# w_down in block products with sums by VectorE, gated factors stored as hi and lo, two weight sums of gate and up by adding transfers

## The chip, the cores and the metric

One core of a Trainium2 chip runs the whole kernel as one program. The metric is device microseconds (us) of that core. An execution under the profiler gives the span from the first to the last instruction, and its own time beside it.

## What is computed

An encoder block for 512 tokens of width 2048 in float32: a normalisation, eight projections, four mLSTM heads and eight differential attention heads, an output projection, and then the gated channel mixer that this case is about. Its width D_FF is 5632.

```python
x = x + jnp.concatenate([hm, ha], axis=-1) @ w_out[l]
h2 = rmsnorm(x, norm2_g[l])
x = x + (jax.nn.silu(h2 @ w_gate[l]) * (h2 @ w_up[l])) @ w_down[l]
return rmsnorm(x, final_g)
```

## The kernel before, in words

**Three matmuls for one.** Every float32 factor is split into a rounded half `hi` and a rest `lo` (`split`, L96): ScalarE (ACT) casts it (L98), VectorE (DVE) subtracts (L99). `three` (L157) then multiplies hi by hi, hi by lo and lo by hi on TensorE (PE). Weights arrive by transfers of SyncE's queue (SP) as tiles of 128 x 1024 in the ring `raw` (7 buffers) and are split into the rings `whi` and `wlo` (3 buffers each), two factors ahead of the product that uses them (`factor`, L921).

**Gate and up.** For each of 22 blocks of 256 features, `group` (L961) runs once for w_gate and once for w_up: 44 groups. A group is a 2 x 2 block product in Winograd's form: seven products P1, P6, P7, P5, P2, P4, P3 of 24 matmuls (128 x 256 out, L931 to L933), with sums around them. `left_factors` (L851) makes the seven weight factors of a group: it loads the four blocks (L856), forms four sums with VectorE (L871, L872, L873, L881) and yields each factor split. `after` (L974) adds the products up with VectorE (L972). `up` (L1032) multiplies with the silu of the gate. For the first 16 blocks it forms four more sums (L1043 to L1046) and writes seven variants of the gated factor to the HBM tensor `actv` by transfers of GpSimd's queue (POOL; L1048, L1049). The last 6 blocks go to `actd` (L1035).

**Down.** w_down's first 4096 rows are worked in 8 units u = (ci, dg), four parts of rows by two halves of columns, in a loop at L1069. A unit is seven products of 24 matmuls (128 x 512 out, L1067, recorded at L158 to L160); each product takes two weight factors, h = 0 and 1, of 12 matmuls each. `load` (L885) fetches the two plain blocks and makes three block sums by a transfer and a second, adding one of GpSimd's queue (L889, L891); two more sums are VectorE's (L913, L915). The left factors are the variants: `variant` (L946) loads one as float32 into a ring `ra` of 2 buffers (L956) and splits it, in the odd units (dg = 1) one product's worth for the next ci beside each product. Products are added over ci into the tiles `M` (L1088 by ScalarE for ci = 0, then L1090 by VectorE).

**The end.** `combine` (L1097) forms the output from the `M` tiles and adds the residual by adding transfers (L1106). The last 1536 rows of w_down are plain products: four blocks by `proj_tok` (L162, called at L1198) and two in the last loop (L1212), which also normalises and stores.

A scheduler sets the order of each engine's instructions; each engine and each queue then works in that order.

Of the kernel before, what the change touches and what calls it, by code (L numbers as in the profile page):

```python
# [30 lines left out]
def build(nc, tc, ctx, a, out):  # L31
# [11 lines left out]
    pacc = pool("acc", 4, space=bass.MemoryType.PSUM)  # L43
    paux = pool("aux", 4, space=bass.MemoryType.PSUM)
# [23 lines left out]
    def tacc():  # L68
        return pacc.tile([128, 512], F32, tag="acc", name=nm("acc"))

    def taux():
        return paux.tile([128, 512], F32, tag="aux", name=nm("aux"))
# [763 lines left out]
    actd = dram.tile([NFB, 2, 128, 512], F32, name="actd")  # L836
    actv = dram.tile([4 * NSP, 7, 128, 256], F32, name="actv")
# [7 lines left out]
    DOWN = ["P1", "P3", "P6", "P5", "P7", "P4", "P2"]  # L845
# [5 lines left out]
    def left_factors():  # L851
        def loads(w, g):
            r = []
            for q in range(4):
                t = tW("raw", bufs=7)
                nc.sync.dma_start(t, a[w][g, q])  # L856
                r.append(t)
            return r
# [8 lines left out]
        for i in range(len(todo)):  # L867
            w11, w12, w21, w22 = nxt
            yield parts(w11)
            s1 = tW("raw", bufs=7)  # L870
            V.tensor_tensor(s1, w21, w22, ALU.add)  # L871
            V.tensor_tensor(w21, w11, w21, ALU.subtract)  # L872
            V.tensor_tensor(w11, s1, w11, ALU.subtract)  # L873
            yield parts(w11)
            yield parts(w21)
# [5 lines left out]
            V.tensor_tensor(w12, w12, w11, ALU.subtract)  # L881
# [3 lines left out]
        def load(u, h, i, ring):  # L885
            j, n, j2, n2 = ((0, 0, 0, 0), (1, 1, 1, 1), (0, 0, 0, 1), (1, 1, 0, 1), (1, 0, 1, 0))[i]
            ci, dg = divmod(u, 2)
            t = ring()
            nc.sync.dma_start(t, a["w_ds"][ci, dg, j, n, h])  # L889
# [4 lines left out]
        order = [(u, i, h) for u in range(2 * NSP) for i in range(5) for h in range(2)]  # L894
# [3 lines left out]
        def upto(k):  # L898
            while pos[0] < min(k, len(order)):
                u, i, h = order[pos[0]]  # L900
                got[u, i, h] = load(u, h, i, tR if h and (u, i) != (0, 0) else lambda: tW("raw", bufs=7))
                pos[0] += 1

        upto(2)
        for u in range(2 * NSP):
            k = 10 * u
            for pi, name in enumerate(DOWN):
                if u or pi:
                    upto(k + (14 if pi == 0 else 16 if pi < 6 else 20))
                for h in range(2):  # L910
                    B11, B22, T1, T3, B21 = (got.get((u, i, h)) for i in range(5))
                    if name == "P6":
                        V.tensor_tensor(B22, B22, T1, ALU.add)  # L913
                    if name == "P4":
                        V.tensor_tensor(B22, B22, B21, ALU.add)  # L915
                    yield parts({"P1": B11, "P3": B22, "P6": B22, "P5": T1, "P7": T3, "P4": B22, "P2": B21}[name])
# [28 lines left out]

    def variant(ci, name, into):  # L946
# [3 lines left out]
        for h in range(2):  # L950
            if more:
                r = more[2].tile([128, 512], F32, tag="ra", name=nm("ra"), bufs=2)
            else:
                r = tW("raw", bufs=7)[:, 0:512]
            g0 = 4 * ci + 2 * h
            nc.sync.dma_start(r.rearrange("p (g c) -> p g c", g=2), actv[g0:g0 + 2, v].rearrange("g p c -> p g c"))  # L956
            hi, lo = tA(), tA()
            split(hi, lo, r)
            into[name].append((hi, lo))

    def group(scale, done, first=False, last=False):  # L961
# [11 lines left out]

        def after(name):  # L974
            if name == "P1":
                SC.copy(ps[:, L], banks[name])
            if name == "P6":
                add(u[:, L], name, ps[:, L])
            if name == "P7":
                add(u[:, R], name, u[:, L])  # L980
            if name == "P5":
                add(C2[:, R], name, u[:, R])
                add(ps[:, R], name, u[:, L])
            if name == "P2":
                add(C1[:, L], name, ps[:, L])
            if name == "P4":
                add(C2[:, L], name, u[:, R])
# [36 lines left out]
    for g in range(NFB):  # L1024
# [7 lines left out]
        def up(i, t):  # L1032
            V.tensor_tensor(t, t, sl[i], ALU.mult)
            if g >= 4 * NSP:
                G.dma_start(actd[g, i], t)  # L1035
# [16 lines left out]
        group(None, up, last=g == NFB - 1)  # L1052


    late[0].close()
    mst, (pM,) = stage(("mm", 1),)
    more.extend(stage(("rr", 1), ("ra", 1)))
    more[1:] = more[1]
    M = [{}, {}]

    def product_down(banks, w, name, h):
        for m in range(2):
            rs = slice(m * 512, m * 512 + 512)
            hi, lo = got_v[name][h]
            for tt in range(2):
                ts = slice(m * 256 + tt * 128, m * 256 + tt * 128 + 128)
                three(banks[tt], hi[:, ts], lo[:, ts], w[0][:, rs], w[1][:, rs], h == 0 and m == 0, h == 1 and m == 1)  # L1067

    for u in range(2 * NSP):  # L1069
        ci, dg = divmod(u, 2)  # L1070
        got_v = cur_v
        if dg == 1:
            cur_v = {}
        for pi, name in enumerate(DOWN):
            if u == 0 and pi < 3:
                variant(0, DOWN[4 + pi], cur_v)
            if dg == 1 and ci + 1 < NSP:
                variant(ci + 1, name, cur_v)
            banks = [tacc(), taux()]
            for h in range(2):  # L1080
                product_down(banks, factor(), name, h)
# [245 lines left out]
```

## Time and profile before

| | us |
|---|---|
| median of 3 runs (2181.03 to 2182.97) | 2181.36 |
| the profiled execution, its own time | 2190.05 |
| span of the profiled execution | 2188.3 |
| PE busy | 2142.0 |
| DVE busy | 1569.6 |
| ACT busy | 992.7 |
| POOL busy | 133.8 |

The profiled execution's own time is 1.75 us longer than its span. The profile counts a matmul as busy until its modelled end, so PE's busy time includes matmuls that run at a lower granted clock. Registers, semaphores and the waiting of the queues are not busy time. By the products' lines, gate and up run from about 800 us to 1693 us, the units of w_down to about 2043 us, and the rest to the end.

### The profile page before, as it was taken

What the parts mean: (1) busy time and instruction counts of PE and PEld (TensorE: products, weight loads), DVE (VectorE), ACT (ScalarE), POOL (GpSimd) and SP (SyncE); (2) the same over time, 40 slices, a digit from 0 to 9 for tenths busy, and PEclk for the clock granted to TensorE, in tenths of its full rate; (3) what the DMA queues carried; (4) which work ended last, traced back from release to release, by engine and by line L of the source; (5) the groups of instructions that cost most, each with busy time, mean ns of one, the idle gap of its engine ahead of it and who ended that gap; (6) DMA issues with size and microseconds to landing.
All of it is one profiled execution on the core that took longest, in us unless ns stands there. A gap on an engine that the chain in (4) does not pass through costs nothing.

```text
span 2188.3 us, 33437 instructions
## 1 busy us (share of the span) xinstructions
PE 2142.0 (98%) x13305; PEld 1938.2 (89%) x13305; DVE 1569.6 (72%) x2362; ACT 992.7 (45%) x1515; POOL 133.8 (6%) x189
## 2 busy tenths in 40 slices
PE   9999999999999999999999999999999799999998
PEld 7888889988888889999999999999999577778786
DVE  6267776366544468888888888888889467779745
ACT  6256675355434354344344443343444454444423
POOL 0011110000000000000000000000000000001100
PEclk9999999999999999999999999999999999999999
DMA  6232112332234424343443434433335986876732
GB/s 257 96 96 78 62 53 72 116 97 87 82 112 146 140 92 131 124 145 119 129 135 119 137 121 133 131 123 117 121 121 168 284 228 184 242 210 156 203 106 77
DMA packets 100749, 292.56 MB, mean 134 GB/s; under 512 B 10976, under 2 KB 27376, under 8 KB 100592
## 3 DMA queue, kind: packets, MB, share of 16 engines
q1 hardware_dynamic: 86832, 247.42, 34.5%
q0 software_dynamic: 13760, 43.00, 8.4%
q8 instruction: 104, 1.70, 0.3%
q14 instruction: 53, 0.43, 0.1%
HBM read 264.16 MB, written 26.22 MB: 133 GB/s over the span
## 4 chain that ended last, share of the span: by engine, by line
PE 85%; DMA 6%; DVE 6%; ACT 2%; issue 1%; ACTq 0%; POOL 0%; DVEq 0%; SPq 0%; POOLq 0%
PE acc L159 9%; PE acc L158 9%; PE acc L160 9%; PE acc L933 8%; PE acc L932 8%; PE acc L931 8%; PE aux L933 6%; PE aux L932 6%; PE aux L931 6%; DMA ra<-actv 4%; PE acc L189 4%; PE acc L190 4%; PE acc L191 4%; DVE wlo L99 2%; PE aux L160 1%
## 5 line engine op out<-in xcount | busy, mean ns | idle before, releaser
L98 ACT CAST whi<-raw 128x1024 fp32r<-128x1024 f32 (+2 forms) x573 | 593.6, 1037 | 807.4 <-PE acc L932 238.8
L99 DVE TENSOR_TENSOR wlo<-raw,whi 128x1024 fp32r<-128x1024 f32 (+2 forms) x573 | 690.5, 1206 | 305.8 <-ACT whi L98 295.0
L158 PE MATMUL acc<-whi,A 128*128 128x512 f32 (+1 forms) x1056 | 404.0, 384 | 21.4 <-ACT whi L98 18.2
L159 PE MATMUL acc<-wlo,A 128*128 128x512 f32 (+1 forms) x1056 | 403.7, 382 | 9.5 <-DVE wlo L99 9.5
L160 PE MATMUL acc<-whi,A 128*128 128x512 f32 (+1 forms) x1056 | 400.7, 379 | 0.0
L158 PEld LDWEIGHTS acc<-whi,A 128*128 128x128 f32 x1056 | 200.0, 190 | 59.4 <-ACT whi L98 22.5
L159 PEld LDWEIGHTS acc<-wlo,A 128*128 128x128 f32 x1056 | 200.3, 190 | 48.0 <-DVE wlo L99 15.0
L160 PEld LDWEIGHTS acc<-whi,A 128*128 128x128 f32 x1056 | 200.4, 190 | 34.0
L932 PE MATMUL acc<-A,whi 128*128 128x256 f32 x704 | 199.3, 283 | 0.5 <-DVE A L99 0.5
L931 PE MATMUL acc<-A,whi 128*128 128x256 f32 x704 | 199.4, 283 | 0.0
L931 PE MATMUL acc<-h,whi 128*128 128x256 f32 x704 | 199.4, 283 | 0.0
L933 PE MATMUL acc<-h,wlo 128*128 128x256 f32 x704 | 199.2, 283 | 0.0
L932 PE MATMUL acc<-h,whi 128*128 128x256 f32 x704 | 199.2, 283 | 0.0
L933 PE MATMUL acc<-A,wlo 128*128 128x256 f32 x704 | 199.2, 283 | 0.0
L933 PE MATMUL aux<-h,wlo 128*128 128x256 f32 x528 | 149.7, 284 | 0.8 <-DVE wlo L99 0.8
L931 PE MATMUL aux<-h,whi 128*128 128x256 f32 x528 | 149.6, 283 | 0.6 <-ACT whi L98 0.6
L189 PE MATMUL acc<-A,whi 128*128 128x512 f32 x384 | 150.1, 391 | 0.0
L190 PE MATMUL acc<-A,whi 128*128 128x512 f32 x384 | 149.8, 390 | 0.0
L191 PE MATMUL acc<-A,wlo 128*128 128x512 f32 x384 | 149.8, 390 | 0.0
L933 PE MATMUL aux<-A,wlo 128*128 128x256 f32 x528 | 149.4, 283 | 0.0
L931 PE MATMUL aux<-A,whi 128*128 128x256 f32 x528 | 149.4, 283 | 0.0
L932 PE MATMUL aux<-A,whi 128*128 128x256 f32 x528 | 149.4, 283 | 0.0
(280 smaller groups left out, 4123.9 us busy)
## 6 DMA issues: line engine op xcount, KB each, us to landing
raw<-in_w_g_dram SPq DMA_DIRECT2D x88, 512.0 KB, 3.5
raw<-in_w_u_dram SPq DMA_DIRECT2D x88, 512.0 KB, 3.6
raw<-in_w_ds_dram SPq DMA_DIRECT2D x80, 512.0 KB, 5.1
raw<-in_w_aqk_dram SPq DMA_DIRECT2D x32, 512.0 KB, 3.4
raw<-in_w_o_dram SPq DMA_DIRECT2D x32, 512.0 KB, 3.5
raw<-in_w_ds_dram POOLq DMA_DIRECT2D x32, 512.0 KB, 8.2
raw<-in_w_b_dram SPq DMA_DIRECT2D x31, 512.0 KB, 4.0
actv<-x POOLq DMA_DIRECT2D x48, 256.0 KB, 3.4
```

The costliest lines, as they stand in the source:

```text
L98: SC.copy(hi, src)
L99: V.tensor_tensor(lo, src, hi.bitcast(F32), ALU.subtract)
L158: PE.matmul(acc, lh, rh, start=first, stop=False)
L159: PE.matmul(acc, lh, rl, start=False, stop=False)
L160: PE.matmul(acc, ll, rh, start=False, stop=last)
L189: PE.matmul(banks[f], wh[:, cs], xh[k], start=first, stop=False)
L190: PE.matmul(banks[f], wh[:, cs], xl[k], start=False, stop=False)
L191: PE.matmul(banks[f], wl[:, cs], xh[k], start=False, stop=last)
L931: PE.matmul(bank, w[0][:, cs], hi, start=m == 0, stop=False)
L932: PE.matmul(bank, w[0][:, cs], lo, start=False, stop=False)
L933: PE.matmul(bank, w[1][:, cs], hi, start=False, stop=m == 7)
```

## The change

1. Gate and up: two of a group's four weight sums are no longer VectorE's. `s1` and `s3` are made by a transfer of SP's queue and an adding one of POOL's into the same tile; the signs of the sums are turned so that only additions are needed. A group now loads five tiles and adds into two of them. VectorE keeps two sums (L879, L887 of the changed file). In the built program a group's s3 takes, of the seven `raw` buffers, the one that the previous group's s3 left; its load can start when that one has been split.
2. The gated factors: each variant, and each of the last 6 blocks, is split into hi and lo when it is made (`halves`, `keep`, L1045 to L1078), and both halves are stored in HBM. The pieces of work wait in a list `later` and run after P1, P6, P7 and P2 of the following group.
3. Down: `variant` loads hi and lo straight into the tiles that the products read, 28 tiles for each ci out of a ring of 38. A table NEXT sets beside which product. No adding transfer is left here: each unit loads four blocks of two tiles and VectorE makes four sums (L916). The order of the products is P1, P5, P3, P7, P2, P6, P4.
4. P1 is added over ci in PSUM (`p1`) and never copied out; the other products use two pairs of banks (`pair`), each copied or added in one instruction of 1024 columns (L1148, L1150).
5. The end: the four blocks for `proj_tok` are loaded during the last units, already split; `combine` becomes a generator in four steps for each half; the splits of the last weights are spread over more steps.

```diff
@@ acc and aux were fixed pools of 4 PSUM banks each @@
+    psum = list(banks_of(("acc", 4), ("aux", 4)))
...
@@ def left_factors(): @@
-            for q in range(4):
+            for q, q2 in ((0, None), (2, 3), (0, 2), (1, None), (3, None)):
                 t = tW("raw", bufs=7)
                 nc.sync.dma_start(t, a[w][g, q])
+                if q2 is not None:
+                    G.dma_start(t, a[w][g, q2], accum_op=ALU.add)
                 r.append(t)
...
-            w11, w12, w21, w22 = nxt
+            w11, s1, s3, w12, w22 = nxt
             yield parts(w11)
-            s1 = tW("raw", bufs=7)
-            V.tensor_tensor(s1, w21, w22, ALU.add)
-            V.tensor_tensor(w21, w11, w21, ALU.subtract)
-            V.tensor_tensor(w11, s1, w11, ALU.subtract)
+            V.tensor_tensor(w11, w11, s1, ALU.add)
             yield parts(w11)
-            yield parts(w21)
+            yield parts(s3)
             yield parts(s1)
             if i + 1 < len(todo):
                 nxt = loads(*todo[i + 1])
             yield parts(w12)
             yield parts(w22)
-            V.tensor_tensor(w12, w12, w11, ALU.subtract)
+            V.tensor_tensor(w12, w12, w11, ALU.add)
             yield parts(w12)
...
-            j, n, j2, n2 = ((0, 0, 0, 0), (1, 1, 1, 1), (0, 0, 0, 1), (1, 1, 0, 1), (1, 0, 1, 0))[i]
...
-            if (j, n) != (j2, n2):
-                G.dma_start(t, a["w_ds"][ci, dg, j2, n2, h], accum_op=ALU.add)
+            j, n = ((0, 0), (0, 1), (1, 1), (1, 0))[i]
+            t = tR() if (h if u else i > 1) else tW("raw", bufs=7)
+            nc.sync.dma_start(t, a["w_ds"][u // 2, u % 2, j, n, h])
             return t
...
+        upto(4)
         for u in range(2 * NSP):
...
-                    upto(k + (14 if pi == 0 else 16 if pi < 6 else 20))
+                    upto(8 * u + (8, 8, 8, 10, 10, 12, 14)[pi])
...
+                    t, o = {"P1": (B11, None), "P5": (B11, B12), "P3": (B22, None), "P7": (B12, B22),
+                            "P2": (B21, None), "P6": (B11, B22), "P4": (B21, B11)}[name]
+                    if o is not None:
+                        V.tensor_tensor(t, t, o, ALU.add)
+                    yield parts(t)
...
@@ def variant(ci, name, into): @@
-            nc.sync.dma_start(r.rearrange("p (g c) -> p g c", g=2), actv[g0:g0 + 2, v].rearrange("g p c -> p g c"))
-            hi, lo = tA(), tA()
-            split(hi, lo, r)
-            into[name].append((hi, lo))
+            into[name].append((tAA(), tAA()))
+            for p in range(2):
+                nc.sync.dma_start(into[name][h][p].bitcast(F32), actv[p, v, 2 * ci + h])
...
@@ def after(name): @@
+            if later and name in ("P1", "P6", "P7", "P2"):
+                later.pop(0)()
...
@@ def up(i, t): @@
+            def halves(t):
+                hi, lo = tX(F32R)[:, :t.shape[1]], t.bitcast(F32R)
+                split(hi, lo, t)
+                return hi, lo
...
-            for k, t in ((0, C1), (2, C2), (4, Sa)):
-                G.dma_start(actv[g, k:k + 2].rearrange("v p c -> p v c"), t.rearrange("p (v c) -> p v c", v=2))
-            G.dma_start(actv[g, 6], Sb[:, L])
+            def keep(k, t, g=g, cs=cs):
+                for p, r in enumerate(halves(t)):
+                    r = r.bitcast(F32)
+                    if k == 6:
+                        G.dma_start(actv[p, 6, g // 2, :, cs], r)
+                    else:
+                        G.dma_start(actv[p, k:k + 2, g // 2, :, cs].rearrange("v p c -> p v c"),
+                                    r.rearrange("p (v c) -> p v c", v=2))
+            later.extend(partial(keep, k, t) for k, t in ((0, C1), (2, C2), (4, Sa), (6, Sb[:, L])))
...
@@ the loop over u @@
+    psum[0].close()
+    pst, (pP1,) = banks_of(("p1", 2))
+    psum[:] = banks_of(("pair", 2))
+    chunks = [Gated(4 * NSP, CHUNKS[0]), Gated(4 * NSP + CHUNKS[0], CHUNKS[1])]
+    NEXT = {(0, 3): 0, (0, 5): 1, (1, 1): 2, (1, 2): 3, (1, 3): 4, (1, 4): 5, (1, 5): 6}
...
-            if dg == 1 and ci + 1 < NSP:
-                variant(ci + 1, name, cur_v)
-            banks = [tacc(), taux()]
+            nxt = NEXT.get((dg, pi))
+            if nxt is not None:
+                if ci + 1 < NSP:
+                    variant(ci + 1, DOWN[nxt], cur_v[1])
+                elif nxt < CHUNKS[0]:
+                    chunks[0].more(tAA)
...
+            if name == "P1":
+                continue
             if ci == 0:
...
-            for tt in range(2):
-                cs = slice(tt * 512, tt * 512 + 512)
-                if ci == 0:
-                    SC.copy(t[:, cs], banks[tt])
-                else:
-                    V.tensor_tensor(t[:, cs], banks[tt], t[:, cs], ALU.add)
+                SC.copy(M[dg][name], bank)
+            else:
+                V.tensor_tensor(M[dg][name], bank, M[dg][name], ALU.add)
```

GpSimd's queue in the gate and up stage, over one gate group and one up group. Before, the four stores of one block are all that it holds:

```order
L1048 DMA actv<-x_8517 128x2x256
L1048 DMA actv<-x_8744 128x2x256
L1048 DMA actv<-x_8516 128x2x256
L1049 DMA actv<-x_8745 128x256
```

After, four adding transfers (raw_8128 and raw_8131 are s1 and s3 of a gate group, raw_8375 and raw_8378 those of the up group) stand among eight stores:

```order
L865 DMA raw_8128<-in_w_g_dram 128x1024
L865 DMA raw_8131<-in_w_g_dram 128x1024
L865 DMA raw_8375<-in_w_u_dram 128x1024
L1075 DMA actv<-x_8332 128x2x256
L1075 DMA actv<-x_8367 128x2x256
L1075 DMA actv<-x_8064 128x2x256
L1075 DMA actv<-x_8065 128x2x256
L865 DMA raw_8378<-in_w_u_dram 128x1024
L1075 DMA actv<-x_8414 128x2x256
L1075 DMA actv<-x_8293 128x2x256
L1073 DMA actv<-x_8481 128x256
L1073 DMA actv<-x_8294 128x256
```

The adding transfer of an up group's s3 now stands behind four stores of the previous block.

VectorE in an odd unit of the down stage, before (wlo: a weight's split, A from ra: a variant's split, M: a product added up, raw from raw: a weight sum):

```order
L99 TENSOR_TENSOR wlo_19393<-raw_19054,whi_19392 128x1024
L913 TENSOR_TENSOR raw_19054<-raw_19054,raw_19094 128x1024
L99 TENSOR_TENSOR A_19429<-ra_19426,A_19428 128x512
L99 TENSOR_TENSOR wlo_19409<-raw_3135_19056,whi_19408 128x1024
L1090 TENSOR_TENSOR M_18129<-acc_19384,M_18129 128x512
L1090 TENSOR_TENSOR M_18129<-aux_19385,M_18129 128x512
L99 TENSOR_TENSOR A_19435<-ra_19432,A_19434 128x512
L99 TENSOR_TENSOR wlo_19442<-raw_19054,whi_19441 128x1024
```

After, at the start of a unit (the last product of the unit before is M_18690; raw_19053 is B11, raw_19143 B12, raw_19191 B22 of h = 0):

```order
L105 TENSOR_TENSOR wlo_19236<-raw_19053,whi_19235 128x1024
L916 TENSOR_TENSOR raw_19053<-raw_19053,raw_19143 128x1024
L916 TENSOR_TENSOR raw_19143<-raw_19143,raw_19191 128x1024
L105 TENSOR_TENSOR wlo_19252<-raw_3085_19055,whi_19251 128x1024
L1150 TENSOR_TENSOR M_18690<-pair_19230,M_18690 128x1024
L105 TENSOR_TENSOR wlo_19270<-raw_19053,whi_19269 128x1024
L916 TENSOR_TENSOR raw_3085_19055<-raw_3085_19055,raw_3105_19145 128x1024
L916 TENSOR_TENSOR raw_19053<-raw_19053,raw_19191 128x1024
L916 TENSOR_TENSOR raw_3105_19145<-raw_3105_19145,raw_3116_19193 128x1024
L105 TENSOR_TENSOR wlo_19287<-raw_3085_19055,whi_19286 128x1024
```

The variants' splits are gone from VectorE's row of work, and the weight sums stand ahead of splits that an earlier product needs.

SyncE's queue where the gate and up stage ends. After (A: halves of the first variants, raw_17966 and raw_17968: B12 of the first unit, raw_2879 to raw_2882: its B22 and B21):

```order
L963 DMA A_17928<-actv 128x512
L894 DMA raw_17966<-in_w_ds_dram 128x1024
L894 DMA raw_17968<-in_w_ds_dram 128x1024
L963 DMA A_18001<-actv 128x512
...
L963 DMA A_18121<-actv 128x512
L894 DMA raw_2879_18079<-in_w_ds_dram 128x1024
L894 DMA raw_2880_18081<-in_w_ds_dram 128x1024
L894 DMA raw_2881_18083<-in_w_ds_dram 128x1024
L894 DMA raw_2882_18085<-in_w_ds_dram 128x1024
```

The first unit's B22 now stands behind the load of A_18121, a tile that the last product of the gate and up stage still reads.

## Rows read from the trace of the kernel before

**Rows 1.** Page: span, busy time of the engines

```profile
span 2188.3 us, 33437 instructions
PE 2142.0 (98%) x13305; PEld 1938.2 (89%) x13305; DVE 1569.6 (72%) x2362; ACT 992.7 (45%) x1515; POOL 133.8 (6%) x189
```

**Rows 2.** Windows: us, then PE, PEld, DVE, ACT, POOL busy, PEclk, DMA share, GB/s

```profile
1000.00:1200.00 200.00, 200.00 (x1669) 200.00 (x1668) 174.70 (x219) 81.42 (x90) 13.54 (x20) 1.00 0.41 129
1691.60:1991.60 300.00, 272.21 (x1130) 218.19 (x1130) 215.70 (x238) 135.64 (x167) 28.47 (x34) 0.95 0.80 225
1691.60:2179.00 487.40, 456.82 (x1935) 370.31 (x1934) 339.93 (x403) 211.99 (x284) 42.32 (x50) 0.96 0.67 191
1691.60:1730.00 38.40, 30.43 (x131) 24.30 (x131) 18.65 (x19) 12.92 (x17) 7.74 (x10) 0.91 1.01 304
```

**Rows 3.** Timeline of PE: start us, us; the down stage's first, two later, a last

```profile
1693.24 0.40 PE L158 MATMUL acc<-whi,A 128*128 128x512 f32 x1
...
2075.74 0.39 PE L160 MATMUL acc<-whi,A 128*128 128x512 f32 x1
...
2078.91 0.39 PE L159 MATMUL acc<-wlo,A 128*128 128x512 f32 x1
...
2178.42 0.39 PE L160 MATMUL acc<-A,b 128*128 128x512 f32 x1
```

**Rows 4.** L158 in windows from 1691.6 to 2179

```profile
1691.60:2179.00 487.40, 255.51 (x640) 123.35 (x640) 0.96 0.67 191
```

**Rows 5.** Waits from 1692 to 2000: us in total, times, longest

```profile
PE acc L158 <- ACT whi L98: 18.2, 7, 5.4
PE acc L159 <- DVE wlo L99: 9.5, 10, 2.1
```

**Rows 6.** Chain of waits, 1838 to 1874: start us, us, what

```profile
1838.38 8.56 DMA ra<-actv
...
1849.43 1.22 DVE wlo L99
...
1861.21 9.65 DMA ra<-actv
...
1872.48 1.24 DVE wlo L99
```

**Rows 7.** Groups, 1750 to 1990: busy us, mean ns, idle before, releasers

```profile
L99 DVE TENSOR_TENSOR wlo<-raw,whi 128x1024 fp32r<-128x1024 f32 x78 | 95.1, 1222 | 24.7 <-ACT whi L98 24.3
L98 ACT CAST whi<-raw 128x1024 fp32r<-128x1024 f32 x79 | 83.0, 1051 | 63.2 <-PE aux L160 54.8 <-DVE raw L913 5.1 <-DVE wlo L99 1.7
L99 DVE TENSOR_TENSOR A<-ra,A 128x512 fp32r<-128x512 f32 x40 | 27.5, 687 | 29.5 <-ACT A L98 29.2
L1090 DVE TENSOR_TENSOR M<-acc,M 128x512 f32<-128x512 f32 x32 | 21.9, 685 | 0.5 <-PE acc L160 0.3
L913 DVE TENSOR_TENSOR raw<-raw,raw 128x1024 f32<-128x1024 f32 x12 | 14.7, 1222 | 0.2
```

**Rows 8.** Timeline of ACT, gate and up: two casts that follow each other

```profile
1117.32 1.05 ACT L98 CAST whi<-raw 128x1024 fp32r<-128x1024 f32 x1 [1.78 <-PE acc L932]
1120.24 1.05 ACT L98 CAST whi<-raw 128x1024 fp32r<-128x1024 f32 x1 [1.88 <-PE aux L932]
```

**Rows 9.** Transfers of L891, whole span, then of L889, 1730 to 1990

```profile
L891 POOL DMA_DIRECT2D raw<-in_w_ds_dram x32: 844/852/891, 1692.0 to 1987.6; - x32
DMA to landing us min/median/max: 5.5/8.2/11.8
...
DMA to landing us min/median/max: 3.4/4.6/9.8
```

**Rows 10.** Group of the stores to actv, 850 to 1760

```profile
L1048 POOL DMA_DIRECT2D actv<-x x47 | 33.5, 713 | 567.7 <-DVE x L1033 509.2 <-DVE x L1046 54.7 <-DVE x L1044 3.6
```

**Rows 11.** Page, DMA queues: packets, MB, share of 16 engines' span

```profile
q1 hardware_dynamic: 86832, 247.42, 34.5%
q0 software_dynamic: 13760, 43.00, 8.4%
```

More of the change, by code (lines that the diff above doesn't have):

```diff
@@ L2 @@
 from contextlib import ExitStack
+from functools import partial
 from itertools import chain
@@ L42, in build, with banks_of @@
     pW = pool("pw", 3)
-    pacc = pool("acc", 4, space=bass.MemoryType.PSUM)
-    paux = pool("aux", 4, space=bass.MemoryType.PSUM)
+    PS = bass.MemoryType.PSUM
+    def banks_of(*pools):
+        st = ExitStack()
+        return st, [st.enter_context(tc.tile_pool(name=n, bufs=b, space=PS, reuse_waits="tile")) for n, b in pools]
+    psum = list(banks_of(("acc", 4), ("aux", 4)))
     dram = pool("dr", 1, space=bass.MemoryType.DRAM)
@@ L944, in build, with tAA @@
     cur_v = {}
+    more_a, nAA = [], [0]
+    def tAA():
+        nAA[0] += 1
+        if (nAA[0] - 1) % 38 < 32:
+            return tA()
+        return more_a[0].tile([128, 512], F32R, tag="aa", name=nm("aa"))
     def variant(ci, name, into):
@@ L972, in add, with less @@
             V.tensor_tensor(out_, banks[name], other, ALU.add)
+        def less(out_, name, other):
+            V.tensor_tensor(out_, banks[name], other, ALU.subtract)
         def after(name):
+            if later and name in ("P1", "P6", "P7", "P2"):
+                later.pop(0)()
             if name == "P1":
@@ L986, in after @@
             if name == "P4":
[L987 removed]
+                less(C2[:, L], name, u[:, R])
                 done(1, C2)
@@ L1177, in last_weights, with evac, at @@
                 yield
-    for ci, nb in enumerate(CHUNKS[:-1]):
-        q = chunks[ci]
-        wait = last_weights()
-        combine(0)
-        for n in range(4):
-            def evac(tt, acc):
-                t = x1[tt][n]
-                V.scalar_tensor_tensor(t, acc, rstd2[:, tt:tt + 1], t, ALU.mult, ALU.add)
-            def at(g):
-                if n == 0:
-                    q.more()
-                if n == 3 and g >= nb - 2:
-                    chunks[ci + 1].more()
-                if n > 0 and g % 2 == 1 and (n, g) != (3, 3):
+    q, nb = chunks[0], CHUNKS[0]
+    wait = last_weights()
+    steps = chain(combine(0), combine(1))
+    for n in range(4):
+        def evac(tt, acc):
+            t = x1[tt][n]
+            V.scalar_tensor_tensor(t, acc, rstd2[:, tt:tt + 1], t, ALU.mult, ALU.add)
+        def at(g):
+            if g < 2:
+                next(steps)
+            if n > 0 and (n, g) != (3, 3):
+                next(wait, None)
+                if n > 1:
                     next(wait, None)
-                if (n, g) == (1, 0):
-                    combine(1)
-            proj_tok(nb, 512, Part(q, 0), Part(q, 1), evac, at)
+            if n == 3 and g >= nb - 2:
+                chunks[1].more(tL)
+        proj_tok(nb, 512, Part(q, 0), Part(q, 1), evac, at)
     for _ in wait:
@@ L1204, in build @@
     nk = 2 * CHUNKS[-1]
-    act.need(nk - 1)
+    while len(act.got) < nk:
+        act.more(tL)
     act = act.got
```

120 lines of the change are left out of this document (59 added, 61 removed).

## The prediction

> **What bounds the kernel now.** I read the page first, then windows by stage, then the waits and the chain inside the stage where PE is not full. The page [rows 1] says that PE is busy for 2142.0 of 2188.3 us, so the first question is where the other 46 us lie, and the second whether the busy time is all at full clock. The windows [rows 2] answer both. In gate and up (1000 to 1200 us as a sample) PE is busy for 200.00 of 200.00 us at clock 1.00: VectorE, at 174.7, hides behind it. From 1691.6 to 2179 us PE is busy for 456.8 of 487.4 us at a mean clock of 0.96, and nearly all of the hole lies before 1991.6, in the units of w_down (272.2 of 300.0, clock 0.95, DMA share 0.80).
>
> How much could come back there? The down stage and the end hold 3 x 640 = 1920 matmuls of 512 columns [rows 4]. Where nothing waits, 14 of them take 2078.91 - 2075.74 = 3.17 us, 0.2264 us each [rows 3]; 1920 take 434.7 us. They really took from 1693.24 to 2178.42 + 0.23, 485.4 us [rows 3]. **The excess is 50.7 us**: 30.6 us of idle PE (487.4 - 456.8) and about 20 us of matmuls at the lower of the clock's two levels, which the windows with idle time show and the full windows do not.
>
> What makes PE wait there? By the waits it is the two halves of a weight split, 18.2 us for ACT's cast and 9.5 us for VectorE's rest [rows 5]. The weight is rarely late itself: the chain [rows 6] runs through loads of `ra`, the variants, of 8.56 and 9.65 us, each followed by work of VectorE. The groups say why: the variants' splits have VectorE idle for 29.5 us ahead of them [rows 7]. VectorE works in order, the variant's split stands between weight splits, its load waits for one of two `ra` buffers, and the weight split behind it comes late.
>
> **Part 1, down without variants' splits and without adding transfers.** A unit is 7 x 24 x 0.2264 = 38.0 us of PE. Before, an odd unit asks of VectorE 14 weight splits and 4 sums of 1.22 us, 14 variant splits of 0.69 and 14 additions to M of 0.685 [rows 7]: 17.1 + 4.9 + 9.7 + 9.6 = 41.3 us, more than PE's. After, every unit asks for 14 splits, 8 sums and 6 additions of two banks, which the trace does not show and which I take as two of 0.685, 1.37 us (the bounds are 1.22, as a sum from SBUF, and 1.37): 17.1 + 9.8 + 8.2 = 35.1 us, 92% of PE's. The order decides whether the 92% suffices. The ten rows shown from the start of a unit hold 4 splits, 5 sums and an addition, 12.3 us, for four factors that PE eats in 4 x 12 x 0.2264 = 10.9 us; the lead of two factors (5.4 us) covers the 1.4 us, and later in the unit VectorE catches up. Transfers: a pair of units loads 16 tiles of 0.524 MB and 28 of 0.262 MB, 15.7 MB in 76 us, 207 GB/s against 225 before [rows 2], none adding, and each is issued at least three products (16 us) ahead, against 9.8 us for the slowest plain load seen [rows 9]. So the 50.7 us should go. **P1 in PSUM** and the wider additions only shorten VectorE's list; they are in the 35.1.
>
> What stays: at the start B22 of the first unit is issued behind A_18121, so when the last product of gate and up ends. VectorE adds B22 ahead of the split of the fourth factor, which PE needs 3 x 2.72 = 8.2 us later; less a sum and a split, the load may take 5.7 us. Loads took 3.4 to 9.8, median 4.6 [rows 9]: 0 to 4 us lost, I take 1. For the hand-over to the plain products I take 1 (0 to 3), and for single late splits 3 over eight units (0 to 3 each, the limit being PE's longest wait for a cast, 5.4 [rows 5]): 5 us stay.
>
> **Part 2, gate and up.** VectorE loses two sums of 1.22 us in a group and gets at most 4 x 0.69 = 2.8 us of halves per two groups; since PE is full, either is worth nothing, as long as PE stays full. What could break it is the s3 tile. A group is 7 products of 24 matmuls, 2.88 us each (1669 in 200 us [rows 2]), 20.2 us. The s3 buffer is free once its split has ended, 2.3 us after its cast began (1.05 [rows 8] + 1.22), so 17.9 us are left until the next s3 is cast; the cast runs two products ahead, and PE itself is held only 3.5 us later. In a gate group: a load of 4.6, an issue of 0.85 and 8.2 until an adding transfer has landed [rows 9], 13.7 us: 4.2 to spare. In an up group POOL has four stores first; they wait for two kept tiles, split behind s1 (2.9 + 2 x 0.69), and take 4 x 0.71 to issue [rows 10]: 7.1 + 0.85 + 8.2 = 16.2 us, 1.7 to spare and 5.2 until PE waits. Cost 0, covered by this lead; bounds 0 and, with the slowest landings of both kinds (9.8 and 11.8 [rows 9], 22.5 us with the issue), 1.1 us of PE in each of 43 groups, 47 us.
>
> Do those landings hold for gate and up, where the trace has no adding transfer? They were taken at a DMA share of 0.80 [rows 2]. A plain MB costs 34.5% of 2188.3 us / 247.42 = 3.05 us of 16 engines, one of POOL's queue 8.4% of it / 43.0 = 4.27 [rows 11]. A group had 0.41 x 20.2 = 8.3 us; a fifth load adds 1.6, two adding ones 4.5, stores twice as large 2.0: 16.4 us, a share of 0.81 and some 230 GB/s. That is the stage in which the landings were measured, below the 1.01 and 304 GB/s of the first 38 us of the down stage [rows 2]. So the median prices are the nearest row. The Trainium skill ("DMA: Bandwidth & Descriptors", section "Issuing engines are not separate DMA queues") speaks against the edit: transfers of all queues run on the same 16 engines and interleave, so a sum handed to POOL is paid by SP's loads. Rows 9 agree in kind: no adding transfer landed in under 5.5 us. With the engines shared the sum is the 0.81 above, still under 1; with engines of their own it would be cheaper; the time is the same by both.
>
> **Sum.** 2190.05 (the profiled execution's own time) - 50.7 + 5 = 2144.4. The median of the runs is 8.7 us below that execution. If this difference lies in the waits that go, the new median is 2144.4; if outside them, 2135.7. I take the middle, **2140 us**.
>
> **The rivals.** *One: gate and up becomes bound by transfers, slower.* Place: s3 of each group. From 4.2 + 3.5 us of lateness in a gate group, or 5.2 in an up group, PE waits in every group, since each s3 waits for the one before. It ends above 2181 when the mean wait passes 45 / 43 = 1.05 us; with the slowest landings throughout, 1.1 x 43 = 47 us, at 2187, and more if gaps lower the clock. For it: DMA share doubles. Against it: the lead and the share of 0.81. Chance 0.11, of which 0.02 ends within 0.2% of no change. *Two: the wait moves.* Sums that stand ahead of splits on VectorE wait for loads (B22 at each unit's start), or SP's queue is held by a variant's tile that PE still reads, and PE waits 3 us more per unit, 24 us in all; about half of the gain is left, 2163 us. For it: L913 and the splits already share VectorE [rows 7] and 92% is little slack. Against it: loads are issued 16 us ahead. Chance 0.12. *Three: the change does nothing for PE* because the casts, not the variants, held it: of the 63.2 us for which ACT's casts wait, 54.8 are for PE to free a buffer [rows 7], so I give it no chance of its own beyond the second.
>
> **How the numbers follow.** The forecast has 0.77. Its bounds: 2135.7 with 5 us less left, and some 2131 if both favours meet; 2144.4 with 10 us more. Reaching to the middle of the second rival leaves out about 2 in 10: 2127 to 2168. About 0.2% (4.4 us) is what a measurement of this kernel can tell from no change. Faster by more: 0.77 + 0.12 = 0.89; within: 0.02; slower: 0.09.
>
> **What would show it.** Right: in gate and up PE still 200 of 200 us with VectorE lower and the DMA share near 0.8; from the first 512-column matmul to the last some 440 us instead of 485, clock 1.00 in the units; no wait of PE for a cast over 2 us except near the start of the units. Wrong: PE waiting for a cast of s3 in gate and up (rival one), a clock below 1.00 there, or VectorE's weight sums waiting for loads in the units (rival two).

## The result, and the profile after

| | before | after |
|---|---|---|
| median of 4 runs, us | 2182.16 (2181.03 to 2185.79) | 2150.41 (2148.33 to 2151.94) |
| the profiled execution, its own time, us | 2190.05 | 2151.25 |

The ratio of the runs is 0.9851, 95% interval 0.9834 to 0.9868: 31.8 us faster. The forecast was 2140 in a range of 2127 to 2168. In the later comparisons the runs of the kernel before lay between 2178.4 and 2192.9; the four of the changed kernel lie within 3.6 us.

The page of the changed kernel, beside [rows 1] and [rows 11]: span and busy times, and the two DMA queues (packets, MB, share of 16 engines).

```profile
span 2149.5 us, 33932 instructions
...
PE 2126.5 (99%) x13305; PEld 1932.3 (90%) x13305; DVE 1504.5 (70%) x2266; ACT 991.2 (46%) x1507; POOL 236.3 (11%) x321
...
q1 hardware_dynamic: 93584, 279.93, 38.0%
q0 software_dynamic: 27392, 90.19, 18.7%
```

Its windows, in the columns of [rows 2]: gate and up, the start of down, the stretch of the units, and the hand-over to the plain products.

```profile
1000.00:1200.00 200.00, 200.00 (x1669) 200.00 (x1668) 164.18 (x219) 91.00 (x110) 45.29 (x60) 1.00 0.80 229
1691.60:1730.00 38.40, 37.40 (x178) 31.35 (x177) 27.82 (x27) 19.74 (x21) 2.17 (x4) 1.00 1.02 386
1691.60:1991.60 300.00, 299.00 (x1333) 248.03 (x1332) 251.81 (x219) 131.29 (x130) 5.70 (x8) 1.00 0.65 219
1990.00:2040.00 50.00, 43.54 (x183) 34.88 (x182) 34.04 (x36) 23.11 (x32) 10.38 (x12) 0.97 0.75 197
```

In gate and up nothing changed for PE: 200.00 of 200.00 us, while the DMA share doubled. In the 300 us of the units PE went from 272.21 to 299.00 at clock 1.00. What is still missing lies after 1990 us. PE's timeline gives the stage as in [rows 3] (start us, us):

```profile
1695.89 0.47 PE L164 MATMUL p<-whi,A 128*128 128x512 f32 x1 [1.00 <-issue]
...
2139.95 0.39 PE L166 MATMUL acc<-b,A 128*128 128x512 f32 x1
```

From the first 512-column matmul to the last one's end it is 2139.95 + 0.23 - 1695.89 = 444.3 us, against 485.4 before and 434.7 without any wait. The 1.00 us of idle time in the first line lies ahead of this stretch. PE's waits of the changed kernel from 2000 to 2045 us (total, times, longest):

```profile
PE acc L164 <- DVE M L1226: 4.8, 2, 3.5
PE acc L164 <- DVE M L1150: 1.6, 1, 1.6
```

The waits for casts and rests of [rows 5] are gone. PE now waits for PSUM banks that VectorE empties late. VectorE's timeline, and behind it ScalarE's and SyncE's queue, show why (start us, us, and in brackets the idle time ahead and its releaser):

```profile
2021.70 0.69 DVE L105 TENSOR_TENSOR A<-raw,A 128x512 fp32r<-128x512 f32 x1 [3.26 <-ACT A L104]
...
2024.93 1.40 DVE L1226 SCALAR_TENSOR_TENSOR M<-acc,rstd,M 128x512 f32<-128x512 f32 x2
2030.92 0.69 DVE L105 TENSOR_TENSOR A<-raw,A 128x512 fp32r<-128x512 f32 x1 [4.59 <-ACT A L104]
2031.53 0.74 DVE L1226 SCALAR_TENSOR_TENSOR M<-acc,rstd,M 128x512 f32<-128x512 f32 x1
```

```profile
2021.05 0.62 ACT L104 CAST A<-raw 128x512 fp32r<-128x512 f32 x1 [3.86 <-DMA raw<-in_w_d_dram]
...
2030.28 1.14 ACT L104 CAST A<-raw 128x512 fp32r<-128x512 f32 x2 [6.52 <-DMA raw<-in_w_d_dram]
```

```profile
2013.16 0.33 SPq L1211 DMA_DIRECT2D raw<-in_w_d_dram  x1
...
2023.56 0.33 SPq L1211 DMA_DIRECT2D raw<-in_w_d_dram  x1
```

The evacuations (L1226) stand on VectorE's list behind splits of the last weights (`last_weights`), and each of those waits for a load issued 7 to 8 us earlier: asked for at 2013.16 and cast at 2021.05, asked for at 2023.56 and cast at 2030.28.

One correction to the description of the kernel before: its `load` in down fetches three plain blocks and makes two block sums by adding transfers, 7 transfers of 0.5 MB for each half of a unit; VectorE makes the other two.

### The profile page after: what moved, and what is told of

It reads as the page before. It is cut to its first block, busy times and chain, and to the rows that moved or that the text cites. A ratio compares the mean times of both kernels' runs of the same rounds, so it can differ in the third digit from the quotient of the medians.

```text
span 2149.5 us, 33932 instructions
## 1 busy us (share of the span) xinstructions
PE 2126.5 (99%) x13305; PEld 1932.3 (90%) x13305; DVE 1504.5 (70%) x2266; ACT 991.2 (46%) x1507; POOL 236.3 (11%) x321
## 3 DMA queue, kind: packets, MB, share of 16 engines
q0 software_dynamic: 27392, 90.19, 18.7%
## 4 chain that ended last, share of the span: by engine, by line
PE 95%; DVE 2%; ACT 1%; DMA 1%; issue 0%; SPq 0%; ACTq 0%; DVEq 0%
PE acc L165 8%; PE acc L164 8%; PE acc L166 8%; PE acc L934 8%; PE acc L933 8%; PE acc L932 8%; PE aux L934 6%; PE aux L932 6%; PE aux L933 6%; PE pair L165 4%; PE pair L164 4%; PE pair L166 4%; PE acc L195 4%; PE acc L196 4%; PE acc L197 4%; DMA raw<-in_w_d_dram 1%
## 5 line engine op out<-in xcount | busy, mean ns | idle before, releaser
L164 PE MATMUL acc<-whi,A 128*128 128x512 f32 (+1 forms) x816 | 306.8, 377 | 0.8 <-DVE T L288 0.4
L165 PE MATMUL acc<-wlo,A 128*128 128x512 f32 (+1 forms) x816 | 305.5, 374 | 0.0
L166 PE MATMUL acc<-whi,A 128*128 128x512 f32 (+1 forms) x816 | 304.7, 373 | 0.0
L164 PEld LDWEIGHTS acc<-whi,A 128*128 128x128 f32 x816 | 153.4, 188 | 25.3 <-ACT whi L104 0.8
L166 PEld LDWEIGHTS acc<-whi,A 128*128 128x128 f32 x816 | 153.5, 188 | 24.7
L165 PEld LDWEIGHTS acc<-wlo,A 128*128 128x128 f32 x816 | 153.6, 188 | 24.2 <-DVE wlo L105 0.6
L932 PE MATMUL aux<-h,whi 128*128 128x256 f32 x528 | 150.1, 284 | 0.6 <-ACT whi L104 0.6
L933 PE MATMUL aux<-h,whi 128*128 128x256 f32 x528 | 149.8, 284 | 0.0
L932 PE MATMUL aux<-A,whi 128*128 128x256 f32 x528 | 149.7, 284 | 0.0
```

Source lines behind the costliest of these rows:

```text
L164: PE.matmul(acc, lh, rh, start=first, stop=False)
L165: PE.matmul(acc, lh, rl, start=False, stop=False)
L166: PE.matmul(acc, ll, rh, start=False, stop=last)
L932: PE.matmul(bank, w[0][:, cs], hi, start=m == 0, stop=False)
L933: PE.matmul(bank, w[0][:, cs], lo, start=False, stop=False)
```

## The experiments

The kernel before had a median of 2184.7 to 2187.1 us in their comparisons; ratios are to that.

### The down stage's sums and the stored halves, one at a time

**VectorE's sums alone.** The kernel before, with nothing changed but `load`, its order and `DOWN`:

```diff
-            if (j, n) != (j2, n2):
-                G.dma_start(t, a["w_ds"][ci, dg, j2, n2, h], accum_op=ALU.add)
...
+                    if o is not None:
+                        V.tensor_tensor(t, t, o, ALU.add)
```

> The kernel before with the changed kernel's down loads and order of products, so that VectorE makes all four block sums in down, but still splits the gated factors there and still makes all sums of gate and up. Theory: VectorE then has 14 splits x 1.22 + 8 sums x 1.22 + 14 additions x 0.74 = 37 us in a unit of 38 and 9.7 us of the factors' splits more in every second one; it is late by about 9 us in two to three of them, on top of what it lost already: slower than before, 2188 to 2212. Rival (the adding transfers in down held TensorE): faster than before, 2150 to 2165.

Measured: 2149.79 us, ratio 0.9847 (0.9824 to 0.9869), all of the gain. My theory fell and the rival's time came, though this run also changes the order of the products and of the loads. Windows, start and units:

```profile
1691.60:1730.00 38.40, 38.40 (x180) 32.09 (x179) 33.04 (x36) 24.73 (x35) 1.08 (x2) 1.00 0.85 301
1730.00:1970.00 240.00, 236.59 (x1039) 194.42 (x1038) 226.81 (x251) 123.11 (x148) 1.78 (x2) 1.00 0.45 145
```

VectorE is busy for 226.81 of 240 us, splits the factors as before, and PE hardly waits. The overload that I had added up is not there: VectorE's timeline of this run has one instruction's start 1.13 us behind the last where 1.22 is listed, and 0.60 for 0.69.

```profile
1891.45 1.22 DVE L910 TENSOR_TENSOR raw<-raw,raw 128x1024 f32<-128x1024 f32 x1
1892.58 1.22 DVE L99 TENSOR_TENSOR wlo<-raw,whi 128x1024 fp32r<-128x1024 f32 x1
1893.71 0.69 DVE L1085 TENSOR_TENSOR M<-acc,M 128x512 f32<-128x512 f32 x1
1894.32 0.69 DVE L1085 TENSOR_TENSOR M<-aux,M 128x512 f32<-128x512 f32 x1
```

With these, a pair of units asks for 44 x 1.13 + 42 x 0.60 = 74.9 us, and PE takes 76.1.

**The stored halves with the adding transfers.** The changed kernel with `load`, its order and `DOWN` of before, the same diff the other way round. P1 in PSUM, the wider additions and the new end stay in, so it does not try the stored halves by themselves:

> The changed kernel with the down stage's weight loads, products' order and block sums of the kernel before (two of four sums by adding transfers), but the gated factors still stored as hi and lo. Theory (what held TensorE was the splitting of the gated factors on VectorE's list, not the adding transfers): 2147 to 2158; VectorE falls from about 35 to about 30 of each 40 us from 1730 to 1970 and TensorE stays near 40. Rival (the adding transfers in down held TensorE): the time goes back to 2168 to 2182.

Measured: 2163.11 us (2161.99 to 2165.12), ratio 0.991 (0.9882 to 0.9937), between the ranges of the theory and of the rival. Its windows:

```profile
1691.60:1730.00 38.40, 29.17 (x114) 22.87 (x114) 17.53 (x17) 12.12 (x14) 7.46 (x10) 0.87 1.05 330
1730.00:1970.00 240.00, 240.00 (x1061) 198.79 (x1060) 170.96 (x143) 101.89 (x98) 21.96 (x26) 1.00 0.98 304
```

In the units PE is full although the DMA engines are at 0.98; 9 us are lost at the start, where the clock is 0.87. So the edits overlap: for the units either the sums by VectorE or the rest of the change is enough, at the start of down only the sums by VectorE help. Which part of the rest it is, the stored halves or P1 in PSUM and the wider additions, was not tried.

**The start of down by itself.** That run, with the sums of the first unit alone by VectorE:

```diff
+            if u == 0:
+                if i == 3:
+                    return None
+                if i == 2:
+                    j, n, j2, n2 = 0, 1, 0, 1
...
+                        if u == 0:
+                            V.tensor_tensor(B11, B11, B12, ALU.add)
+                            V.tensor_tensor(B12, B12, B22, ALU.add)
```

> The changed kernel with the down stage's adding transfers and order of before, as in the second run, but the first of its eight units makes its sums on VectorE from four plain loads. Theory (the 13 us that the adding transfers cost with the factors stored lie at the start of down, where the units' first factors and weights are all loaded at once and the DMA engines are full): 1690 to 1730 us has TensorE busy for 38 to 40 of 40 us and the time is 2150 to 2156. Rival (they lie in later units or at the hand-over): 2159 to 2165.

Measured: 2151.37 us (2150.75 to 2152.88), the theory's. Its window of the start:

```profile
1691.60:1730.00 38.40, 37.23 (x168) 30.29 (x167) 26.76 (x26) 19.14 (x20) 5.63 (x8) 1.00 1.03 372
```

So 11.7 of the 12.7 us that the adding transfers cost in this kernel come from the first unit. By these medians the other seven units' adding transfers cost the 1.0 us that is left, which is within the spread of the runs.

### What held the units

**No ring for the factors' loads.** The kernel before, each factor loaded into its own tile:

```diff
-                r = more[2].tile([128, 512], F32, tag="ra", name=nm("ra"), bufs=2)
...
+            hi, lo = tA(), tA()
+            r = lo.bitcast(F32)
```

> The kernel before, adding transfers in down and all, but a gated factor of down is loaded straight into the tile of its lower half and split there, so that the two-buffer ring of its loads is gone; its splits stay on ScalarE's and VectorE's lists. Theory, new after the first four runs (inside the units it is the late landing of a factor's load, asked for only when one of two buffers came free, that held both lists; at the start of down it is the transfers themselves): the units lose nothing, the start still about 9 us: 2160 to 2170. Rival (the splits and their place in the lists hold the weights' splits, whenever the factor lands): 2175 to 2187.

Measured: 2190.7 us, ratio 1.003 (1.0018 to 1.0043), 6 us slower and past both ranges. As a test of the landing it says nothing, since the factors land no earlier: SyncE's queue now waits for a product to free the tile. Its waits from 1735 to 1990 us (total, times, longest), the kernel before first, then this run:

```profile
SPq L956 <- DVE A L99: 60.3, 40, 4.6
```

```profile
SPq L954 <- PE aux L160: 38.7, 15, 3.1
```

ScalarE's waits for a factor from 1735 to 1990 us (total, times, longest), the kernel before first, then this run:

```profile
ACT A L98 <- DMA ra<-actv: 62.2, 29, 6.2
```

```profile
ACT A L98 <- DMA A<-actv: 64.5, 31, 9.9
```

What it does show: taking the two buffers away does not help by itself. How much they held back stays open, since another wait took their place.

**The splits later.** That run, with each factor's split one to two products behind its load:

```diff
+            now[0] += 1
+            while owed and owed[0][0] < now[0] - 1:
+                split(*owed.pop(0)[1:])
...
-            split(hi, lo, r)
...
+            if more:
+                owed.append([now[0], hi, lo, r])
```

> The run before it without the two-buffer ring (kernel before, factors loaded straight into their tiles), with each factor's split put one to two products later in the program than its load; transfers, bytes and the work of each engine stay as they were. Theory (inside the units ScalarE's and VectorE's lists stand still at splits whose factor has not landed, which the adding transfers delay; the work of the splits has room): the waits of ScalarE for a factor's load fall from 64 to under 20 us, the units lose little, the start of down still its 9 us: 2158 to 2172. Rival (not the landing but the splits' work, or the weights' own transfers, hold the lists): 2178 to 2192.

Measured: 2156.94 us (2156.34 to 2157.26), ratio 0.9859 (0.9841 to 0.9876), a little under the theory's range: some 34 us below the run it differs from, with the same transfers and the same work. The wait for a factor and the windows:

```profile
ACT A L98 <- DMA A<-actv: 6.6, 3, 3.2
```

```profile
1691.60:1730.00 38.40, 32.52 (x131) 25.75 (x130) 23.68 (x26) 19.07 (x27) 5.45 (x7) 0.87 1.05 329
1730.00:1970.00 240.00, 239.67 (x1058) 198.25 (x1057) 202.06 (x226) 127.69 (x155) 22.99 (x27) 1.00 0.84 241
```

PE is full in the units, and the start is as bad as before. Inside the units it was the place of the splits: the lists of ScalarE and VectorE stood still at a factor that had not landed, with the weights' splits behind it.

**The amount moved.** The run with all sums by VectorE, with three of four blocks transferred a second time, plain, from GpSimd's queue:

```diff
             nc.sync.dma_start(t, a["w_ds"][u // 2, u % 2, j, n, h])
+            if i < 3:
+                G.dma_start(t, a["w_ds"][u // 2, u % 2, j, n, h])
```

> The run in which the kernel before makes all four block sums of down on VectorE, with three of four block loads followed by a second plain transfer of the same block from GpSimd's queue, so that down moves 7 MB in a unit again, as with two sums by adding transfers. It computes the same. Theory (the adding transfers cost TensorE its time by the time they take of the 16 DMA engines, wherever a load is asked for late): DMA share about 1 at the start of down and 0.7 to 0.9 in the units, and the time goes back to 2165 to 2185. Rival (it is the kind of transfer or the order of the products that matters, not the amount moved): 2148 to 2156.

Measured: 2168.5 us (2166.96 to 2178.56), ratio 0.9931 (0.9911 to 0.9951): 18.7 us of the 35 come back.

```profile
1691.60:1730.00 38.40, 29.65 (x123) 23.35 (x122) 27.10 (x31) 17.82 (x26) 5.32 (x10) 0.87 0.97 367
1730.00:1970.00 240.00, 233.14 (x1015) 189.26 (x1014) 218.05 (x239) 121.94 (x149) 19.03 (x36) 1.00 0.66 228
```

At the start PE loses as much as with the adding transfers. The amount moved is not enough to explain it: the changed kernel moves 386 GB/s there, at a share of 1.02, and PE loses nothing behind its first 512-column matmul. What this run has in common with the adding transfers is a second transfer that GpSimd's queue can only issue when the first one into the same tile has landed; from 1690 to 1725 us that queue waited (total, times, longest):

```profile
POOL raw L890 <- DMA raw<-in_w_ds_dram: 15.0, 3, 12.0
```

Whether this chain of two transfers alone costs the 9 us, or only together with full engines, was not tried. In the units PE loses 6.9 us at a share of 0.66, less than the 0.7 to 0.9 that I had expected. The same window of the kernel before:

```profile
1730.00:1970.00 240.00, 220.19 (x906) 175.99 (x905) 176.73 (x198) 114.28 (x143) 18.19 (x22) 0.95 0.78 220
```

With adding transfers it is 19.8 us, and ScalarE's wait for `ra` is 34.2 us against 25.9 without the second transfers and 62.2 before. The loads of `ra` show the same order, from 1735 to 1990 us: before, with VectorE's sums alone, and in this run:

```profile
DMA to landing us min/median/max: 2.6/3.9/10.0
```

```profile
DMA to landing us min/median/max: 2.5/3.5/5.4
```

```profile
DMA to landing us min/median/max: 2.4/3.6/7.3
```

The second transfers are no full stand-in for the adding ones. GpSimd's queue from 1730 to 1970 us, before and in this run (packets, MB, share of 16 engines):

```profile
q0 software_dynamic: 3163, 11.52, 26.7%
```

```profile
q0 software_dynamic: 5185, 18.88, 21.8%
```

By these rows a MB took 5.6 us of the 16 engines with adding (26.7% of 240 us for 11.52 MB) and 2.8 us without. How much of the rest is due to this price and how much to the order of products and loads, which also differs, stays open.

### Gate and up

**Its adding transfers alone.** The kernel before with `loads`, `left_factors` and the signs of `after` as changed:

```diff
-            for q in range(4):
+            for q, q2 in ((0, None), (2, 3), (0, 2), (1, None), (3, None)):
...
+                if q2 is not None:
+                    G.dma_start(t, a[w][g, q2], accum_op=ALU.add)
```

> The kernel before with two of the four sums of gate and up by adding transfers and nothing else of the change. Theory (this part is worth nothing by itself: TensorE was busy without a gap there): 2177 to 2187, as before; VectorE from 1000 to 1200 us falls by about 24 us, the DMA share rises from 0.41 to 0.7 to 0.8. Rival one of the prediction (the transfers bound gate and up): over 2190. Second rival (VectorE was in the way there as well): under 2172.

Measured: 2185.28 us against 2185.52, ratio 1.0002 (0.9987 to 1.0017): worth nothing, and harmless. VectorE falls by 19 us, less than expected, and PE stays full:

```profile
1000.00:1200.00 200.00, 200.00 (x1669) 200.00 (x1668) 155.53 (x199) 81.35 (x90) 31.29 (x40) 1.00 0.74 205
```

**The changed kernel without them.** Four plain loads and four sums by VectorE:

```diff
+            s1 = tW("raw", bufs=7)
+            V.tensor_tensor(s1, w21, w22, ALU.add)
+            V.tensor_tensor(w21, w11, w21, ALU.add)
+            V.tensor_tensor(w11, s1, w11, ALU.add)
```

> The changed kernel with all four block sums of gate and up made by VectorE again, from four plain loads; the down stage as changed. Theory (the gain lies in the down stage; the adding transfers of gate and up only took work off an engine that had room): from 1000 to 1200 us VectorE rises from 164 to about 188 of 200 us, the DMA share falls from 0.80 to 0.5 to 0.6, TensorE stays at 200 of 200, and the time is that of the changed kernel, 2150, within 2147 to 2157. Rival (with hi and lo of the gated factors split there too, VectorE no longer has room for the two sums): TensorE waits in gate and up and the time is 2165 to 2200.

Measured: 2150.63 us (2150.31 to 2152.5), as the changed kernel. Its window has VectorE at 183.81 and the DMA share at 0.46, both a little under what was expected:

```profile
1000.00:1200.00 200.00, 200.00 (x1669) 200.00 (x1668) 183.81 (x240) 91.27 (x110) 27.07 (x40) 1.00 0.46 152
```

**More traffic there.** A first try with copies that nothing reads:

```diff
+            for q in range(2):
+                nc.sync.dma_start(sink[q], a[w][g, q])
```

> The changed kernel with two 0.5 MB copies from DRAM to DRAM more in each group of gate and up (88 groups of 7 products, 20.2 us each with its pair; nothing reads them). It measures how much room the transfers of gate and up left, the price of rival one of the prediction: by the DMA rows of before 1 MB takes 2.9 to 4.5 us of the 16 engines, read and written perhaps twice that, on top of 0.80 of the stretch. Theory (TensorE is held there only when the DMA share reaches about 1): with a share up to 0.95 the time stays within 2150 to 2158; with a share of 0.98 and more TensorE waits and the time grows by the excess, by up to 100 us. Rival (any more traffic delays the chain of a sum by two transfers): over 2165 with a share still under 0.95.

Measured: 2153.7 us, but the test failed: the scheduler put all 88 copies between 42 and 279 us, ahead of gate and up (count, duration, first and last start):

```profile
L869 SPq DMA_DIRECT2D sink<-in_w_g_dram x44: 488/488/606, 42.2 to 274.3; - x44
L869 SPq DMA_DIRECT2D sink<-in_w_u_dram x44: 488/488/834, 48.5 to 279.1; - x44
```

A second try ties the traffic to the blocks:

```diff
+                elif q in (1, 3):
+                    G.dma_start(t, a[w][g, q])
```

> The changed kernel with two of the three plain blocks of each group of gate and up (the ones for the fifth and sixth product) transferred a second time from GpSimd's queue, as the sums' blocks are but without adding: 1 MB more in each of 44 groups. It computes the same. It tests the price of rival one of the prediction: 16.1 us of the DMA engines' time in a group of 20.2 become about 20.4. Theory (a transfer costs TensorE time where it is asked for late; gate and up ask for their blocks most of a group ahead, so they lose only what goes past the full engines): DMA share 0.95 to 1.03, time 2150 to 2170. Rival (the chain of a sum by two transfers has too little slack for more traffic, as rival one had it): 1 to 3 us in every group, 2195 to 2280.

Measured: 2151.29 us (2149.89 to 2151.99), nothing lost. The share is 0.91, under what was expected, and PE full:

```profile
1000.00:1200.00 200.00, 200.00 (x1669) 200.00 (x1669) 164.96 (x218) 90.61 (x110) 55.59 (x79) 1.00 0.91 282
```

### The hand-over, and a faster version

The changed kernel with the last weights loaded one step ahead of their splits, in even steps:

```diff
+                held.append((n, r))
+                if len(held) > 1:
+                    parts_of(*held.pop(0))
                 yield
...
-            if n > 0 and (n, g) != (3, 3):
+            if (n, g) > (0, 1):
                 next(wait, None)
-                if n > 1:
-                    next(wait, None)
```

> The changed kernel with the last chunk's weights loaded one step ahead of their splits, in even steps from the third granule of the first plain column block on. Theory (the 9.6 us lost around 2000 to 2036 us are evacuations that stand on VectorE's list behind splits whose load was asked for one step before): the loss falls to 1 to 4 us: 2141 to 2146. Rival (the ring of seven weight buffers is what the loads wait for, so that the wait only moves to the last products of the units): 2149 to 2156.

Measured: 2143.69 us (2142.97 to 2145.28), ratio 0.9808 (0.9792 to 0.9825), 6.7 us below the changed kernel and the fastest of all. The window of the hand-over, against 43.54 at clock 0.97:

```profile
1990.00:2040.00 50.00, 48.65 (x213) 39.41 (x212) 36.97 (x41) 26.18 (x37) 10.36 (x12) 1.00 0.94 263
```

The same with the steps starting at the second column block (`if n > 0:`):

> As the run before, but the steps start with the first granule of the second plain column block, after the evacuations of the first in program order. Theory: as there, 2141 to 2146, and no split of these weights ahead of the units' last additions. Rival (the ring of seven weight buffers): 2149 to 2156.

Measured: 2146.93 us (2145.7 to 2147.36), ratio 0.9821 (0.9805 to 0.9838): 3.5 us below the changed kernel, half of it, and a little past the range. So the splits' place was the cause of most of the loss; why the late start gives only half was not looked into.

## Why the prediction was right, and where not

The forecast's own case came in: down lost its excess, gate and up stayed full. Set against the profiled execution, 2144.4 was expected of the sum and 2151.25 came. The difference is 4.6 us more left in down (9.6 instead of 5), and 2.65 us by which down starts later, less 0.3 us behind the last matmul.

**The excess of 50.7 us.** Its size and place were right: 41.1 of it went. The lowered clock went with the idle time, as argued: 1.00 in the units.

**Its cause in the units.** "VectorE works in order, the variant's split stands between weight splits" was right; the run with the splits put later shows it. "Its load waits for one of two `ra` buffers" did not hold up as the cause: without the ring nothing got better. But the run without the ring waits for another tile instead, so the ring's part is not shown. Without the adding transfers the slowest of these loads landed in 5.4 us instead of 10.0, in a run with another order of loads; the prediction removed those transfers in the same breath and did not price them. The 41.3 us that VectorE was to need in an odd unit, "more than PE's", was wrong: durations listed back to back overlap, and at the measured spacing it is 18 x 1.13 + 28 x 0.60 = 37.1, under 38.0. With that the storing of halves was taken for a needed half of the gain; the sums by VectorE, with their order of products and loads, bring all of it without it.

**VectorE after.** 35.1 us in a unit, 92%, was forecast. The units' window has 251.81 of 300 us, 84%. The addition from two banks, taken as 1.37, was listed at 1.22, its lower bound:

```profile
L1150 DVE TENSOR_TENSOR M<-pair,M 128x1024 f32<-128x1024 f32 x33 | 40.3, 1222 | 7.0 <-PE pair L166 6.5
```

**What stays.** Start of down: 1 us was forecast for B22's load, and the only idle time there is the 1.00 us ahead of the first 512-column matmul, where PE waited for nothing that the profile shows. That the numbers agree is luck; from that matmul on nothing was lost, at a DMA share of 1.02. Single late splits in the units: 3 forecast, none seen. **The step that failed** is "for the hand-over to the plain products I take 1 (0 to 3)": nearly all of the 9.6 us lies there, 6.4 of it in the waits shown above, the rest in matmuls at the lower clock (0.97 on average from 1990 to 2040 us). I had looked at the units' transfers, not at which splits the scheduler puts ahead of an evacuation.

**Part 2.** Cost 0, share 0.81 and some 230 GB/s were forecast; 0.80 and 229 were measured. That the share came out is in part luck. GpSimd's queue from 1000 to 1200 us, with all four sums by VectorE and then as changed:

```profile
q0 software_dynamic: 2880, 9.18, 11.7%
```

```profile
q0 software_dynamic: 5746, 19.61, 42.2%
```

The two adding transfers took 30.5% of a group's 20.2 us, 6.2 us where 4.5 was priced; the larger stores (11.7% against 7.3% before, 0.9 us where 2.0 was priced) and the fifth load (37.0% against 33.8% of SyncE's queue, 0.6 us where 1.6 was priced) made up for it. Rival one's border also has a slip: from the forecast of 2140 it is 41 / 43 = 0.95 us a group to 2181, not 45 / 43; nothing hung on it. Rival one had little behind it: with 1 MB more in each group PE still did not wait. The rule of the Trainium skill ("DMA: Bandwidth & Descriptors", "Issuing engines are not separate DMA queues"), that transfers of all queues interleave on the same 16 engines, shows itself at the start of down instead: with the adding transfers in, SyncE's plain loads of weights issued from 1690 to 1730 us land late. First the run with stored halves and adding transfers, then the changed kernel (count, KB each, median us to landing):

```profile
raw<-in_w_ds_dram SPq DMA_DIRECT2D x8, 512.0 KB, 20.4
```

```profile
raw<-in_w_ds_dram SPq DMA_DIRECT2D x18, 512.0 KB, 7.5
```

**The median.** Half of the 8.7 us by which the profiled execution lay above the median was taken off. That was wrong: after, execution and median differ by 0.8 us. The 8.7 lay, as far as these runs tell, in the waits that went and that vary from run to run, so 2144.4 was the better reading. Rival two had the right kind of event, a wait that moves to VectorE's list, at another place and some 9 us instead of 24.

## What to carry to other kernels

Before an engine's list is made shorter, look whether it stands still: a split or sum that waits for a load holds all that is behind it, and putting it later was worth as much in the units as removing it. A stage with full DMA engines need not lose anything: PE was full at a share of 0.98 in the units and of 1.02 at the start of down. It lost at the start where a weight needed a second transfer behind the first. When several edits aim at one stall, try each alone: here the sums by VectorE, with their order, brought the whole gain.

## What the runs showed beyond that

- Back to back, VectorE's instructions of 128 x 1024 listed at 1.22 us start every 1.13 us, those of 128 x 512 listed at 0.69 every 0.60. Sums of listed durations overstate a full list by 8 to 15%.
- Plain transfers moved 386 GB/s at a DMA share of 1.02 (start of down, after); with adding ones in, 304 at 1.01 [rows 2]. With plain second transfers instead it was 367 at 0.97, and PE lost as much.
- An adding transfer took the 16 engines 5.6 us per MB in the units of the kernel before and 5.8 in gate and up (30.5% of 200 us for 10.43 MB more), a plain one of the same queue 2.8. The prediction's 4.27 was a mean over everything that the queue moved.
